# Hybrid two-layer encoder on one core: the first pass started from one row of c, with warm-up products on TensorE

## The chip, the cores and the metric

The kernel runs on one core of a Trainium2 chip. The core has five engines with an instruction queue each: TensorE (PE, with its weight loads shown apart as PEld), VectorE (DVE), ScalarE (ACT), GpSimd (POOL) and SyncE (SP), which here issues all DMA transfers. Each engine takes its instructions in the order in which the program was built; semaphores hold an instruction until what it needs is there. The metric is the device time of one execution in microseconds.

## The reference

The input x has 1024 tokens of 1024 features; c is one vector of 1024. Two layers follow each other, each with a modulation by c, and a last normalisation:

```
for i in range(2):
    mod = silu(c) @ ada_w[i] + ada_b[i];  shift, scale, gate = split(mod, 3)
    h = rmsnorm(x, norm_g[i]) * (1 + scale) + shift
    y = diff_attention(h, positions, ...) if i == 0 else mla(h, positions, ...)
    x = x + gate * y
return rmsnorm(x, final_norm_g)
```

Layer 0 projects h to q, k, v and z (each 1024 wide), turns q and k by rope (cosines and sines of position times frequency), forms two softmax maps per head (8 heads), subtracts lambda times the second, and gates by silu(z). Layer 1 is latent attention. All is float32.

## The kernel before

A float32 product on TensorE is made of three (`mm3`, lines 183 to 186): each operand is split into a high part in fp32r (a ScalarE copy) and a low part (a subtraction on GpSimd or VectorE), and high x high, high x low and low x high are added up in PSUM.

The first pass is what the change touches. The tokens are two halves of four tiles of 128. For the first half the kernel must have c: line 424 loads it spread to 128 partitions (512 KB) on SP's queue, ahead of the four tiles of x (line 524). ScalarE and VectorE form twice silu(c) (lines 427, 428) and ScalarE copies it into PSUM as `cb` (line 559). Squares of x (lines 534 on ScalarE, 537 on VectorE) lead to one root for the four tiles (`inv_rms`, line 465, GpSimd's power at line 171); ScalarE scales the first 256 features of each tile (line 567), VectorE the rest (line 621).

Then a loop goes over eight chunks k of 128 features. `mod_pair` multiplies two loaded tiles of ada weights (512 KB each, tag `ada`, four buffers) with `cb` and sums (line 434): the shift and scale of the chunk. `h_chunk` (line 479) transposes the chunk of the four token tiles on TensorE (line 488), ScalarE applies scale and shift twice (lines 493 to `h0h`, 495 to `h`), GpSimd subtracts (line 498) to `h0l`. `load_wv` (line 543) loads a chunk of value weights (tag `wvr`, two buffers) and splits it (lines 547, 548); every fourth chunk a strip of key weights (`wraw`, lines 208, 229, 230) is split too. Fifteen matmuls a chunk (lines 638 to 644) add to four value accumulators and one key accumulator: ten with `h0h`, then five with `h0l`. The matmuls of chunk k are issued one turn later than its `h_chunk` (`SKEW`).

Within the loop the second half of x is loaded (`X1_AT`), and the query weights (`WQ_AT`). In the last turn `angles()` runs: nine VectorE steps on a 128 x 256 tile, a table load and three sines on ScalarE, and three stores; `load_tables` brings the cosine and sine tables back in the layout of rope. After the loop the second half is squared and scaled, the query strip of the first half is multiplied, and the second half goes through the same chunks (lines 184 to 186 for its value matmuls). Then follow the value projection of the other heads (`vps`), the key and query strips of the second half, and the attention.

What sets the order: the program text gives work to the engines, and a list scheduler, by its own costs, orders each engine's queue when the program is built. `tc.issue_after(x)` keeps what is written under it behind x. The order is fixed before the kernel runs.

Of the kernel before, what the change touches and what calls it, by code (L numbers as in the profile page):

```python
# [11 lines left out]
F32 = mybir.dt.float32  # L12
# [52 lines left out]
WQ_AT = 6  # L65
# [3 lines left out]
X_CUT = 256  # L69
FIN_LAG = 1  # L70
# [15 lines left out]
def trunk(ctx: ExitStack, tc: tile.TileContext, A, out):  # L86
# [329 lines left out]
    def mod_load(src, mp, nb, tag="ada"):  # L416
        w = mp.tile([P, D], F32, name="ada", tag=tag, bufs=nb)
        SP.dma_start(w, src)
        return w

    def load_c(pl, th, **kw):

        c2 = pl.tile([P, D], F32, name="c2", **kw)
        SP.dma_start(c2, A["c"].to_broadcast([P, D]))

        def fin():
            S.activation(th, c2, AF.Tanh, scale=0.5)
            V.scalar_tensor_tensor(out=c2, in0=th, scalar=1.0, in1=c2, op0=ALU.add, op1=ALU.mult)

        return c2, fin  # L430
# [48 lines left out]
    def h_chunk(l, xn4, k, dst, hp, sub=G, wide=False, act=False, f32=None):  # L479
# [13 lines left out]
        S.activation(hh, tr[:, :n, :], AF.Identity, bias=bk, scale=ak)  # L493
        if act:
            S.activation(tmp, tr[:, :n, :], AF.Identity, bias=bk, scale=ak)
        else:
            V.tensor_scalar(tmp, tr[:, :n, :], ak, bk, op0=ALU.mult, op1=ALU.add)
# [16 lines left out]
    def load_x(half):  # L514

        xs = []
        for j in range(4):
            if half == 1 and j > 1:
                xs.append([wp.tile([P, HF], F32, name="xth", tag="rp", bufs=6) for _ in range(2)])
            else:  # L520
                xs.append([p1.tile([P, D], F32, name="xt", tag="xt", bufs=6)])
            for i, x_ in enumerate(xs[j]):
                n = D // len(xs[j])
                SP.dma_start(x_, A["x"][half * 4 + j, :, i * n : i * n + n])
        return xs

    def sq_x(xs, on_act=range(4)):
        ss = sm.tile([P, 4], F32, name="xss")
        for j, x_ in enumerate(xs):
            for i, piece in enumerate(x_):  # L530
                dst = ss[:, j : j + 1] if i == 0 else sm.tile([P, 1], F32, name="xs2")
                if j in on_act:
                    junk = p1.tile([P, D], BF16, name="junk", tag="junk", bufs=1)
                    S.activation(junk[:, : piece.shape[1]], piece, AF.Square, accum_out=dst)
                else:
                    junk = p1.tile([P, D], BF16, name="junk2", tag="h32", bufs=2)
                    V.tensor_tensor_reduce(out=junk, in0=piece, in1=piece, scale=1.0, scalar=0.0, op0=ALU.mult, op1=ALU.add, accum_out=dst)
                if i:
                    V.tensor_add(ss[:, j : j + 1], ss[:, j : j + 1], dst)
        return ss  # L540

    def load_wv(l, k, fh, src, eng=G):
        raw = p1b.tile([P, HF], F32, name="wvr", tag="wvr", bufs=2)
        SP.dma_start(raw, src)
        h_ = p1b.tile([P, HF], F32R, name="wvh", tag="wv", bufs=16)
# [5 lines left out]
    psum("ps1", accx=3, tr=1, cb=1)  # L551
    th = p1.tile([P, D], F32, name="cth", tag="ada", bufs=ADA_B)
    c2, c_fin = load_c(p1b, th)
    xs0 = load_x(0)
    posi = p1.tile([P, 256], I32, name="posi", tag="rot", bufs=3)
    SP.dma_start(posi, A["pos"])
    c_fin()
    cb = bank("cb", "cb", [P, D])
    S.copy(cb, c2)

    def ada0(j):
        return [mod_load(A["ada_ss0"][j, i], p1, ADA_B) for i in range(2)]

    wm0 = ada0(0)
    y0 = inv_rms(sq_x(xs0, X_ACT0), 4)
    for j in range(4):
        S.mul(xs0[j][0][:, :X_CUT], xs0[j][0][:, :X_CUT], y0[:, j : j + 1])


    tabS = [dr.tile([4, 32, 256], F32, name=f"tabS{i}") for i in range(3)]  # L570

    def angles():
        ang = p1.tile([P, 256], F32, name="ang", tag="rot", bufs=3)
        kk = p1.tile([P, 256], F32, name="kk", tag="rot", bufs=3)
# [12 lines left out]
        nsin = p1.tile([P, 256], F32, name="nsin", tag="h32", bufs=2)  # L587
        S.activation(kk, ang, AF.Sin, scale=0.5)
        S.activation(nsin, ang, AF.Sin, scale=-1.0)
        S.activation(ang, ang, AF.Sin)  # L590
        V.tensor_mul(kk, kk, kk)
        V.tensor_scalar(kk, kk, -2.0, 1.0, op0=ALU.mult, op1=ALU.add)
        for d_, s_ in zip(tabS, (kk, nsin, ang)):
            SP.dma_start(d_.rearrange("b p t -> (b p) t"), s_)
# [15 lines left out]
    for k in range(-1, KT + SKEW):  # L610
        if k + 1 < KT:
            wm = wm0 if k < 0 else ada0(k + 1)
            wv0.append(load_wv(0, k + 1, 0, A["w_v0"][k + 1, 0]))
            if k % 4 == 0:
                for d_, w_ in zip(wk0, load_strip([A["w_s0"][1, 0, k // 4]], [4])):
                    d_ += w_
            m_last = mod_pair(0, k + 1, wm, cb)
        if k < 0:
            with tc.issue_after(m_last):
                for j in range(4):  # L620
                    V.tensor_scalar(xs0[j][0][:, X_CUT:], xs0[j][0][:, X_CUT:], y0[:, j : j + 1], None, op0=ALU.mult)
        if k == KT - 1:
            with tc.issue_after(m_last):
                angles()
        if k == X1_AT:
            xs1 = load_x(1)
# [1216 lines left out]
```

## Time and profile before

| | us |
|---|---|
| runs | 1444.38, 1444.8, 1437.6 (median 1444.38) |
| the profiled execution | 1438.65 |
| its span | 1436.9 |
| TensorE busy | 1388.8 (97%) |
| VectorE, ScalarE, GpSimd busy | 917.5, 728.7, 610.6 |
| TensorE idle before its first transpose | 14.5 |

The profile is of one execution. A line of the timeline gives the start and the duration in microseconds, the engine, the program's line, the operation and its tiles (out, then in); what stands in brackets is the idle time in front of it and what ended it. Lines joined with xN follow each other without a break. A line of stretches gives its bounds and length, then busy time and number of instructions of PE, PEld, DVE, ACT and POOL, the granted clock, the busy share of the DMA engines and GB/s. A line of waits gives the total, the number and the longest. Matmuls are pipelined: their durations overlap, and the distance of two starts is what one costs.

### The profile page before, as it was taken

What the parts mean: (1) busy time and instruction counts of PE and PEld (TensorE: products, weight loads), DVE (VectorE), ACT (ScalarE), POOL (GpSimd) and SP (SyncE); (2) the same over time, 40 slices, a digit from 0 to 9 for tenths busy, and PEclk for the clock granted to TensorE, in tenths of its full rate; (3) what the DMA queues carried; (4) which work ended last, traced back from release to release, by engine and by line L of the source; (5) the groups of instructions that cost most, each with busy time, mean ns of one, the idle gap of its engine ahead of it and who ended that gap; (6) DMA issues with size and microseconds to landing.
All of it is one profiled execution on the core that took longest, in us unless ns stands there. A gap on an engine that the chain in (4) does not pass through costs nothing. (4 is left out here: it accounts for less than half of the span.)

```text
span 1436.9 us, 20644 instructions
## 1 busy us (share of the span) xinstructions
PE 1388.8 (97%) x7388; PEld 1158.8 (81%) x7388; DVE 917.5 (64%) x1372; ACT 728.7 (51%) x1287; POOL 610.6 (42%) x483
## 2 busy tenths in 40 slices
PE   5999999999999999998999999999999999999997
PEld 4778788888888888887787877887888888888886
DVE  6656877767777767677435985545666555555355
ACT  5622375666565656566343452335455554545342
POOL 4416164656464646464461343532141331412572
PEclk9999999999999999999999999999999999999999
DMA  8787723333332333237653145398343432336563
GB/s 326 238 254 237 255 70 93 84 104 81 96 101 84 96 89 91 86 96 248 236 183 125 38 132 184 122 305 236 133 130 111 130 101 77 104 96 217 185 237 136
DMA packets 135527, 213.70 MB, mean 149 GB/s; under 512 B 19072, under 2 KB 56064, under 8 KB 135424
## 3 DMA queue, kind: packets, MB, share of 16 engines
q1 hardware_dynamic: 135424, 212.38, 47.1%
q8 instruction: 58, 0.95, 0.3%
q14 instruction: 45, 0.37, 0.1%
HBM read 137.92 MB, written 50.80 MB: 131 GB/s over the span
## 5 line engine op out<-in xcount | busy, mean ns | idle before, releaser
L384 ACT CAST pth<-tr 128x512 fp32r<-128x512 f32 x256 | 150.6, 588 | 284.2 <-PE tr L382 281.9
L399 DVE TENSOR_REDUCE nm<-s 128x1 f32<-128x1024 f32 x192 | 234.1, 1219 | 77.2 <-PE s L773 65.7
L385 DVE TENSOR_TENSOR ptl<-tr,pth 128x512 fp32r<-128x512 f32 x256 | 176.2, 688 | 139.4 <-ACT pth L384 138.9
L230 POOL TENSOR_TENSOR wl<-wraw,wh 128x512 fp32r<-128x512 f32 (+2 forms) x79 | 103.6, 1314 | 205.6 <-ACT wh L229 183.4
L401 ACT ACTIVATE e<-s,nm 128x1024 f32<-128x1024 f32 x128 | 143.7, 1123 | 29.8 <-DVE nm L399 29.2
L382 PE MATMUL tr<-ident,e 128*128 128x128 f32 x1024 | 155.1, 274 | 2.3 <-DVE ptl L385 2.0
L382 PEld LDWEIGHTS tr<-ident,e 128*128 128x128 f32 x1024 | 121.2, 140 | 43.6 <-DVE ptl L385 19.2
L184 PE MATMUL acc<-h0h,wh 128*128 128x512 f32 x360 | 150.1, 417 | 1.9 <-DVE v_hl L362 1.8
L184 PE MATMUL pv<-pth,vt 128*128 128x256 f32 x512 | 147.1, 287 | 0.0
L185 PE MATMUL pv<-ptl,vt 128*128 128x256 f32 x512 | 145.8, 285 | 0.0
L186 PE MATMUL pv<-pth,vt 128*128 128x256 f32 x512 | 144.7, 283 | 0.0
L186 PE MATMUL acc<-h0h,wl 128*128 128x512 f32 x360 | 143.1, 398 | 0.5 <-POOL wl L230 0.5
L185 PE MATMUL acc<-h0l,wh 128*128 128x512 f32 x360 | 142.0, 394 | 0.0
L1013 POOL TENSOR_TENSOR wol<-wor,woh 128x512 fp32r<-128x512 f32 x64 | 85.0, 1351 | 84.7 <-ACT woh L1012 77.2
L185 PEld LDWEIGHTS pv<-ptl,vt 128*128 128x128 f32 x512 | 97.6, 191 | 2.9
L184 PEld LDWEIGHTS pv<-pth,vt 128*128 128x128 f32 x512 | 97.4, 190 | 2.9 <-ACT pth L384 0.2
L186 PEld LDWEIGHTS pv<-pth,vt 128*128 128x128 f32 x512 | 97.6, 191 | 0.1
L326 POOL TENSOR_TENSOR rp_r<-rp_raw,cosT 128x512 f32<-128x512 f32 x38 | 49.8, 1311 | 91.0 <-ACT rp_raw L321 50.8
L331 POOL TENSOR_TENSOR rp_sw<-rp_sw,sinT 128x512 f32<-128x512 f32 x42 | 55.4, 1318 | 74.1 <-DMA rp_sw<-rp_raw 73.9
L773 PE MATMUL s<-ks,qa 128*128 128x512 f32 x256 | 82.6, 404 | 2.8 <-DVE e L781 2.6
L781 DVE SCALAR_TENSOR_TENSOR e<-s,z,e 128x1024 f32<-128x1024 f32 x64 | 82.1, 1283 | 2.1
L773 PE MATMUL s<-ks,qb 128*128 128x512 f32 x256 | 81.1, 395 | 0.0
(590 smaller groups left out, 3335.4 us busy)
## 6 DMA issues: line engine op xcount, KB each, us to landing
ada<-in_ada_ss SPq DMA_DIRECT2D x32, 512.0 KB, 6.0
wraw<-in_w_s SPq DMA_DIRECT2D x64, 256.0 KB, 2.9
vS<-v_hl SPq DMA_DIRECT2D x32, 512.0 KB, 5.9
vt<-vS SPq DMA_DIRECT2D x32, 512.0 KB, 3.7
wor<-in_w_out SPq DMA_DIRECT2D x64, 256.0 KB, 3.9
rp_sw<-rp_raw SPq DMA_DIRECT2D x168, 64.0 KB, 2.0
bc_s<-bc_d SPq DMA_DIRECT2D x34, 256.0 KB, 4.1
oS<-bc_s SPq DMA_DIRECT2D x30, 256.0 KB, 2.5
```

The costliest lines, as they stand in the source:

```text
L184: PE.matmul(psum, ah, bh, start=first, stop=False)
L185: PE.matmul(psum, ah, bl, start=False, stop=False)
L186: PE.matmul(psum, al, bh, start=False, stop=last)
L230: sub = (V if pair_of else G).tensor_sub(l_[:, :n], raw[:, :n], f32v(h_[:, :n]))
L382: PE.transpose(tr[:, j, :], p[:, kt * P : (kt + 1) * P], ident)
L384: mk["S"] = S.copy(pth[kh][:, :, dst], tr).ins
L385: mk["V"] = V.tensor_sub(ptl[kh][:, :, dst], tr, f32v(pth[kh][:, :, dst])).ins
L399: mk["V"] = V.reduce_max(nm, s_ps, axis=AX.X, negate=True).ins
L401: mk["S"] = S.activation(e, s_ps, AF.Exp, bias=nm, scale=1.0, accum_out=zs).ins
L773: PE.matmul(s_ps[:, kc * HF : (kc + 1) * HF], src[:, c, ql], KS[h][kc][:, c, :], start=fst, stop=not fst)
L781: combined.append(V.scalar_tensor_tensor(out=e0, in0=e1, scalar=z1[:, 0:1], in1=e0, op0=ALU.mult, op1=ALU.add).ins)
L1013: in_turn(G.tensor_sub(lo, raw, f32v(hi)))
```

## The change

- c is loaded into one partition (`crow`, 4 KB). The tanh and the product with it work on that one row, and two f32 products of a row of ones with it (512 columns each) spread it to 128 partitions of `cb` in PSUM. The layer-1 copy `c2` is now made from `cb` in the loop.
- `keep_busy` adds 40 + 36 f32 products of ones by ones (128 x 128 x 128) into a bank of PSUM that nothing reads.
- The loads are reordered: position after the first tile of x, the first ada tile ahead of the fourth tile of x.
- The first three tiles of x get their root together; the fourth is squared in halves on ScalarE and VectorE and gets its own.
- The angle steps follow the product of c; the three sines stand behind chunks 2 and 3, the cosine's last two steps and the stores behind chunk 6 (`SIN_AT`).
- Value, key and query weights are loaded in one place and split in another, the split behind the chunk's last ScalarE step (`h_chunk.act`). `WQ_AT` goes from 6 to 5.
- The squares of the second half: two tiles on VectorE behind the last shift and scale, two on ScalarE behind the last chunk. Before, ScalarE did all.

In the order as built TensorE gets 55 of the 76 products first, then the two that spread c, then 21, then the first transposes. After the first pass the query strip of the second half now precedes its key strip. The last load of value weights for the next pass (the ninth `wvr`) stands ahead of the ada loads of chunk 7 on SP's queue.

```diff
-WQ_AT = 6
+WQ_AT = 5
+WARM = (40, 36)
+SIN_AT = (2, 3, 6)
...
-        c2 = pl.tile([P, D], F32, name="c2", **kw)
-        SP.dma_start(c2, A["c"].to_broadcast([P, D]))
...
+    warm = bank("acc", "warm")
+
+    def keep_busy(n):
+        for _ in range(n):
+            PE.matmul(warm[:, 0:P], ones, ones, start=True, stop=True)
+
+    crow = p1.tile([P, D], F32, name="crow", tag="ada", bufs=ADA_B)
     th = p1.tile([P, D], F32, name="cth", tag="ada", bufs=ADA_B)
-    c2, c_fin = load_c(p1b, th)
-    xs0 = load_x(0)
+    SP.dma_start(crow[0:1, :], A["c"])
+    xs0 = [load_x(0, 0)]
     posi = p1.tile([P, 256], I32, name="posi", tag="rot", bufs=3)
     SP.dma_start(posi, A["pos"])
-    c_fin()
-    cb = bank("cb", "cb", [P, D])
-    S.copy(cb, c2)
+    xs0 += [load_x(0, 1), load_x(0, 2)]
+    keep_busy(WARM[0])
...
+    wm0 = [ada0(0, 0)]
+    xs0.append(load_x(0, 3))
+    wm0.append(ada0(0, 1))
...
+    c_act = S.activation(th[0:1, :], crow[0:1, :], AF.Tanh, scale=0.5).ins
+    c_last = V.scalar_tensor_tensor(out=crow[0:1, :], in0=th[0:1, :], scalar=1.0, in1=crow[0:1, :], op0=ALU.add, op1=ALU.mult).ins
+    with tc.issue_after(c_last):
+        angles()
+    cb = bank("cb", "cb", [P, D])
+    for f in range(2):
+        fs = slice(f * HF, f * HF + HF)
+        PE.matmul(cb[:, fs], ones[0:1, :], crow[0:1, fs], start=True, stop=True)
+    keep_busy(WARM[1])
...
+    for j in range(3):
+        with tc.issue_after(c_act if j in X_ACT0 else c_last):
+            sq_piece(xs0[j][0], ss0[:, j : j + 1], j in X_ACT0)
+    y_ = inv_rms(ss0[:, 0:3], 3)
...
+    sq_halves([xs0[3][0][:, :HF], xs0[3][0][:, HF:]], ss0[:, 3:4])
+    y0[3] = inv_rms(ss0[:, 3:4], 1)[:, 0:1]
...
+    def sines(n):
+        with tc.issue_after(h_chunk.act):
+            if n == 0:
+                S.activation(kk, ang, AF.Sin, scale=0.5)
+                S.activation(nsin, ang, AF.Sin, scale=-1.0)
+            if n == 1:
+                S.activation(ang, ang, AF.Sin)
+                S.copy(c2, cb)
+        if n == 2:
+            with tc.issue_after(m_last):
+                V.tensor_mul(kk, kk, kk)
+                V.tensor_scalar(kk, kk, -2.0, 1.0, op0=ALU.mult, op1=ALU.add)
+            for d_, s_ in zip(tabS, (kk, nsin, ang)):
+                SP.dma_start(d_.rearrange("b p t -> (b p) t"), s_)
...
-            wm = wm0 if k < 0 else ada0(k + 1)
-            wv0.append(load_wv(0, k + 1, 0, A["w_v0"][k + 1, 0]))
+            wm = wm0 if k < 0 else [ada0(k + 1, i) for i in range(2)]
+            vraw = fetch_wv(A["w_v0"][k + 1, 0])
+            if k < 0:
+                with tc.issue_after(h_chunk.act):
+                    wv0.append(split_wv(vraw))
...
         if 0 <= k < KT:
             h_chunk(0, xs0, k, h0[k][0], p1, act=True)
+            if k + 1 < KT:
+                with tc.issue_after(h_chunk.act):
+                    wv0.append(split_wv(vraw))
+            if k in SIN_AT:
+                sines(SIN_AT.index(k))
...
-    norm_x(sq_x(xs1), xs1)
+    ss1 = sm.tile([P, 4], F32, name="xss")
+    with tc.issue_after(m_last):
+        for j in range(2):
+            sq_piece(xs1[j][0], ss1[:, j : j + 1], False)
+    with tc.issue_after(h_chunk.act):
+        for j in range(2, 4):
+            sx = sm.tile([P, 1], F32, name="xs2")
+            sq_piece(xs1[j][0], ss1[:, j : j + 1], True)
+            sq_piece(xs1[j][1], sx, True)
+            V.tensor_add(ss1[:, j : j + 1], ss1[:, j : j + 1], sx)
+    norm_x(ss1, xs1)
```

123 lines of the change are left out of this document (61 added, 62 removed).

## The prediction

> **What bounds the kernel now.** I read the page's first part, then TensorE's waits, then the busy time of each engine in stretches of the first 120 us, where every edit lies, and at last the timeline there. The issue order of the two programs, laid side by side, differs on all engines only up to about this time.
>
> ```profile
> span 1436.9 us, 20644 instructions
> PE 1388.8 (97%) x7388; PEld 1158.8 (81%) x7388; DVE 917.5 (64%) x1372; ACT 728.7 (51%) x1287; POOL 610.6 (42%) x483
> ...
> PE trh L488 <- ACT xt L567: 14.5, 1, 14.5
> ...
> 0.00:20.90 20.90, 5.53 (x15) 3.53 (x16) 12.19 (x21) 10.52 (x16) 6.43 (x11) 1.00 0.89 333
> 20.90:49.20 28.30, 28.10 (x134) 22.52 (x132) 21.99 (x44) 17.74 (x28) 18.08 (x15) 1.00 0.91 335
> 49.20:55.00 5.80, 3.62 (x8) 2.37 (x9) 2.53 (x6) 4.64 (x13) 1.26 (x1) 0.71 0.61 184
> 55.00:85.00 30.00, 29.57 (x143) 23.84 (x143) 19.51 (x33) 10.35 (x18) 8.63 (x7) 1.00 0.68 199
> 85.00:120.00 35.00, 32.92 (x139) 25.62 (x139) 20.93 (x30) 9.89 (x18) 11.57 (x7) 1.00 0.84 243
> ```
>
> TensorE is busy 97% of the span, so a microsecond counts if TensorE gets it. What the first pass can give is its idle time: 14.5 us before the first transpose, 2.2 us (5.80 less 3.62) around the last chunk, 2.1 us (35.00 less 32.92) later. Between 20.9 and 49.2 TensorE is full (28.10 of 28.30): there the pass can begin sooner but not run faster.
>
> ```profile
> 0.82 0.17 DVE L145 MEMSET ones<- 128x128 f32 x1 [0.82 <-PEq L1832]
> 1.17 0.42 SPq L424 DMA_DIRECT2D c<-in_c  x1
> 6.22 1.06 ACT L427 ACTIVATE cth<-c 128x1024 f32<-128x1024 f32 x1 [4.22 <-DMA c<-in_c]
> 12.87 1.28 DVE L434 CUSTOM_DVE_ANT_0 ada<-ada,cb,vec 128x1024 f32<-128x1024 f32 x1
> 14.46 1.68 PE L488 MATMUL trh<-ident,xt 128*128 128x128 f32 x4 [14.46 <-ACT xt L567]
> 15.43 0.16 DVE L442 SCALAR_TENSOR_TENSOR moda<-moda,vec 128x1 f32<-128x1 f32 x1
> 16.18 0.78 ACT L493 ACTIVATE h0h<-trh,modb,moda 128x512 fp32r<-128x512 f32 x1
> 17.01 0.80 PE L638 MATMUL vacc<-wvh,h0h 128*128 128x512 f32 x1 [0.87 <-ACT h0h L493]
> 20.15 0.63 PE L638 MATMUL vacc<-wvh,h0h 128*128 128x512 f32 x1
> 20.57 0.48 PE L639 MATMUL vacc<-wvl,h0h 128*128 128x512 f32 x1
> 20.89 0.40 PE L638 MATMUL vacc<-wvh,h0h 128*128 128x512 f32 x1
> 23.30 0.50 PE L638 MATMUL vacc<-wvh,h0h 128*128 128x512 f32 x1 [0.18 <-ACT h0h L493]
> 24.09 0.60 PE L488 MATMUL trh<-ident,xt 128*128 128x128 f32 x4
> 36.42 0.40 PE L638 MATMUL vacc<-wvh,h0h 128*128 128x512 f32 x1
> 36.65 0.40 PE L639 MATMUL vacc<-wvl,h0h 128*128 128x512 f32 x1
> 46.74 0.39 PE L638 MATMUL vacc<-wvh,h0h 128*128 128x512 f32 x1
> 51.28 1.93 PE L643 MATMUL vacc<-wvh,h0l 128*128 128x512 f32 x4 [2.10 <-POOL h0l L498]
> 54.75 0.47 PE L186 MATMUL acc<-h0h,wq 128*128 128x512 f32 x1
> 55.06 0.39 PE L184 MATMUL acc<-h0h,wq 128*128 128x512 f32 x1
> ```
>
> Two more costs show. Matmuls start 0.42 us apart at 20.15 to 20.57 and 0.23 apart at 36.42 to 36.65: TensorE is slow from its first work at 14.46 until 20.89 (6.4 us), and again from 51.28 until 54.75 (3.5 us) after the 2.10 us wait. And chunk 1 begins at 23.30, chunk 7 at 46.74: six chunks in 23.44 us, 3.91 each.
>
> **The yardstick.** The fourth matmul of the query strip starts at 55.06. If chunk 0's matmuls begin at S and nothing stalls, it starts at S + 7 x 3.91 + 18 x 0.23 = S + 31.5. So S = 23.6 would change nothing.
>
> **Warm-ups.** 76 f32 products of ones by ones are added. The text asks for 40, the row of c, then 36. In the changed program's issue order 55 stand ahead of the two products that spread c and 21 behind them, and the first transposes come after all. Their price is that of the like-shaped product in the tail:
>
> ```profile
> 703.37 1.13 PE L830 MATMUL rb<-sq,ones 128*128 128x128 f32 x8 [0.93 <-DVE sq L829]
> 704.25 0.48 PE L184 MATMUL oacc<-woh,oth 128*128 128x512 f32 x1
> ...
> 1350.48 1.05 PE L830 MATMUL rb<-dg,ones 128*128 128x128 f32 x8
> 1351.29 0.48 PE L184 MATMUL oacc<-woh,o1a3h 128*128 128x512 f32 x1
> ```
>
> Four products leave eight records, and the next instruction starts 0.88 or 0.81 us later: 0.20 to 0.22 us a product, taken as 0.21. 76 cost 16.0 us (15.4 to 16.7). The two spreading products have four times the columns: 0.84 each, 1.7 together; at the 0.23 of a 512-column record, two records each, it is 0.9. The slow stretch of 3.5 to 6.4 us loses about half: 1.7 to 3.2, taken as 2.5. TensorE can start when the ones are there, 1.0. So c is spread at 1.0 + 55 x 0.21 + 2.5 + 1.7 = 16.8, and the transposes start at T = 16.8 + 21 x 0.21 = 21.2, against 14.46 before (bounds 1.0 + 15.4 + 0.9 + 1.7 = 19.0 and 1.0 + 16.7 + 1.7 + 3.2 = 22.6).
>
> The Trainium skill, "TensorE: Matmul & The Clock Gate", section "Back-to-back issue gap", gives some 81 ns for a sustained matmul of 128 columns. By that estimate 76 cost 6.2 us and T is about 10; the rows above are of this shape and type and say 0.21, and I go by them.
>
> **c as a row.** The 4.6 us from issue (1.59) to use (6.22) of the 512 KB spread load, the copy into PSUM and the 128-row operand go; c is ready no later than there. It then waits behind the warm-ups until 16.8, so this earns nothing. It also holds a buffer: row and tanh take two of the four ada buffers, and the second shift/scale load of chunk 1 waits for the spreading products. Everything behind it on SP's queue waits too (key weights, next value weights, later ada). I expect transfers to run dry before that.
>
> **Shift and scale of chunk 0.** The first pair took 12.87 to 15.59, 2.7 us. Two angle steps now sit inside:
>
> ```profile
> 18.55 0.62 ACT L229 CAST wh<-wraw 128x512 fp32r<-128x512 f32 x1
> 46.36 1.34 DVE L585 SCALAR_TENSOR_TENSOR ang<-kk,ang 128x256 f32<-128x256 f32 x3
> 47.74 0.29 DVE L586 TENSOR_SCALAR ang<-ang 128x256 f32<-128x256 f32 x1
> 40.58 1.29 POOL L548 TENSOR_TENSOR wvl<-wvr,wvh 128x512 fp32r<-128x512 f32 x1 [0.28 <-ACT wvh L547]
> 55.19 0.64 ACT L534 ACTIVATE junk<-xth 128x512 bf16<-128x512 f32 x1
> 59.96 0.38 PE L488 MATMUL trh<-ident,xt 128*128 128x128 f32 x2
> 61.43 0.50 PE L184 MATMUL vacc<-wvh,h0h 128*128 128x512 f32 x1 [0.43 <-ACT h0h L493]
> ada<-in_ada_ss SPq DMA_DIRECT2D x32, 512.0 KB, 6.0
> wraw<-in_w_s SPq DMA_DIRECT2D x64, 256.0 KB, 2.9
> ```
>
> 0.45 + 0.29 more: ready at 16.8 + 3.5 = 20.3, ahead of the transposes (21.2 + 0.60 = 21.8). The key-weight split stands ahead of h0h on ScalarE: 16.8 + 2.9 for the transfer, up to 1.5 more for the 512 KB in front at 335 GB/s, + 0.62 = 20.3 to 21.8, just covered. Then h0h and first matmul, 16.18 to 17.01: S = 21.8 + 0.8 = 22.6 (bounds 20.4 and 24.0). By the yardstick that gains 1.0.
>
> **Last tile, squares, sines, angles.** The separate fourth tile and the angle steps lie on ScalarE and VectorE before 17 and are covered by the warm-ups; were these gone, the angle steps inside the first pair would cost their 0.7. The sines, one table load and the copy of c for layer 1 go between chunks 2 and 5 on ScalarE; each chunk of 3.91 us asks 2.2 us of it (0.78 + 0.78 + 0.62), so they fit in what is left over. This clears the path of the last h32, and the 2.10 us wait with the slow stretch (half of 3.5) goes. That gain is already in the yardstick. What is late next: SP's order puts the value weights of the next pass ahead of chunk 7's shift and scale; their buffer is freed by GpSimd's split of chunk 6. That follows h0l of chunk 5, whose transposes stand at chunk 4: 22.6 + 15.6 + 0.4 + 0.78 + 0.78 = 40.2; GpSimd is then still on the key-weight subtraction (1 us left, I estimate from its three in a row of 1.29), then h0l and the split, 1.29 each: about 43.7. Two stores of sines stand in that stretch of SP's queue too. The two 512 KB loads issue then and land 2.9 to 6.0 later (I take 4.3, the queue being short) and 1.5 more (512 KB at 335 GB/s): 49.5; a product and the scale 1.5, h0h 0.8: chunk 7 starts at 51.8 and not 22.6 + 27.4 = 50.0. A stall of 1.8 (0.3 to 3.5). The yardstick falls at 55.9, 0.8 late (bounds -3.2 with no stall and S 20.4; +5.9 with S 24.0, 3.5 and another 1.8 of slow clock).
>
> **Second half of the tokens.** Its loads follow chunk 7's on SP: 2 MB at 335 GB/s end at 55.8; from the last square to the transposes it took 4.8 us (55.19 to 59.96) and to the first matmul 6.2: 62.0 against 61.43, and the strip, 0.8 late, asks the same. I carry +0.8. The query strip now precedes the key strip, and only 5 of the value matmuls stand before it; weights are wanted later. Of the 2.1 us idle in 85 to 120 I save half (0 to 2.1).
>
> **Sum.** +0.8 - 1.0 = -0.2 on the profiled execution's 1438.65 (span 1436.9 and 1.75 around it): 1438.5. The runs lie on two levels, 1437.6 with the profile and 1444.4 to 1444.8; the median, 1444.38, is 5.7 above it. I name 1441, between 1438.5 and 1444.2, which is the same sum on the median. 0.5% (7.2 us), the spread of these runs, is what a measurement tells from no change.
>
> **Rivals.**
> - Slower: the clock stays shut during f32 products. For it: after the transposes it opened only 3.9 us behind the first fp32r matmul (17.01 to 20.89), and no trace here has f32 products for microseconds on end. Against: 6.4 us from the first transpose fits as well. Then 76 x 0.21 x 0.42 / 0.23 = 29.1, spread 3.1, T = 33.2, S = 34.6, 1.8 more until it opens: 67.9 at the yardstick, with the same stall 69.7, +14.6; less 1.0: 1452.2. Above half that excess it decides. Chance 0.09.
> - Faster: the warm-ups overlap so well that they no longer hold c back. S is then set by the shift and scale; VectorE has more ahead of them than before, so no sooner than 12.87: 12.87 + 3.5 + 0.8 = 17.2, 6.4 gained, 1432. Against it stand both rb rows, where a product would have to cost half. 0.05. (The skill's 81 ns, from the section named above, would do this.)
> - The upper level of the runs comes from the spread load of c, which took 4.6 us for the first bytes; one row of 4 KB ends it. All runs would be near 1438, 0.45% under the median. No row speaks of the upper level. 0.10.
> - Chunk 7's stall at its long end with the slow clock: +5, 1443.7, on the upper level 1449. 0.10.
>
> **How the numbers follow.** The forecast has 0.66. Range 1433 to 1450: it takes in all but the shut clock and the cheap warm-ups (0.14) and some scatter. Faster by over 0.5%: 0.13 (cheap warm-ups, most of the level case with a microsecond gained, little else). Slower: 0.13 (shut clock, some of the long stall). Same: 0.74.
>
> **What would show it.** The first transpose of xt near 21 and the products for cb ending near 17, not 6; warm-up records 0.1 apart after 4 to 8 us; chunk 0 near 22.6; no wait for h0l at chunk 7, but one for its h0h with VectorE waiting for ada; the strip's fourth matmul at 53 to 58. A first chunk before 20 or after 27 would prove the first step wrong.

## The result, and the profile after

The changed kernel takes 1448.47 us (median of 14 runs, 1445.85 to 1450.48); the kernel before, in runs between these on the same chip, 1441.63 us (14 runs, 1437.6 to 1445.33). The ratio is 1.0043, 95% interval 1.0031 to 1.0055: about 6 us slower. That is outside the interval and inside the 0.5% that the prediction had set aside; the forecast of no change (-0.2 us) was wrong. The profiled executions stand 7.9 us apart, 1446.54 (span 1444.8) against 1438.65; the traces below are of these two executions, and show some 1.7 us more than the ratio.

The first part of the page after:

```profile
span 1444.8 us, 20958 instructions
PE 1408.7 (98%) x7544; PEld 1179.8 (82%) x7544; DVE 924.9 (64%) x1378; ACT 725.4 (50%) x1285; POOL 610.2 (42%) x484
```

TensorE is busy 19.9 us longer than before (1408.7 against 1388.8), about what the warm-up products take (14.07 and 6.58 us in the timeline below). Busy time alone says nothing here: the kernel now computes ones by ones.

The busy time of each engine in stretches, after (start:end, length, then PE, PEld, DVE, ACT, POOL, each with its count, the granted clock of TensorE, DMA share and GB/s):

```profile
0.00:20.90 20.90, 19.86 (x136) 18.50 (x137) 10.87 (x29) 7.58 (x13) 3.70 (x9) 0.93 0.73 250
85.00:120.00 35.00, 32.44 (x135) 25.94 (x133) 22.25 (x31) 9.19 (x16) 9.12 (x5) 0.95 0.82 245
120.00:150.00 30.00, 29.40 (x130) 24.03 (x128) 15.78 (x24) 10.12 (x17) 16.62 (x11) 1.00 0.68 203
150.00:180.00 30.00, 24.93 (x108) 19.71 (x109) 22.60 (x35) 8.71 (x15) 0.89 (x1) 1.00 0.91 283
...
17.91:21.32 3.41, 3.41 (x18) 3.41 (x18) 3.41 (x9) 0.00 (x0) 0.00 (x0) 0.50 1.04 295
...
93.00:96.41 3.41, 3.41 (x10) 2.63 (x9) 2.83 (x5) 0.00 (x0) 0.00 (x0) 0.50 0.84 241
```

The same view of before, for the two stretches that the prediction did not look at:

```profile
120.00:150.00 30.00, 30.00 (x134) 24.84 (x133) 20.09 (x31) 9.28 (x16) 14.12 (x9) 1.00 0.85 273
150.00:180.00 30.00, 28.66 (x135) 22.87 (x134) 24.19 (x35) 12.62 (x23) 3.83 (x3) 1.00 0.74 233
```

The last stretch is the surprise: between 150 and 180 us, far behind every edit, TensorE is busy 24.93 us where it was 28.66, with 108 matmul records where there were 135. And within these 180 us the clock, once open, was shut twice for 3.41 us, once among the warm-ups themselves.

The timeline of after at the places that matter (start, length, engine, line, what; in brackets the idle time before it and what ended that; SPq is SyncE's queue of transfers):

```profile
1.04 14.07 PE L551 MATMUL warm<-ones 128*128 128x128 f32 x110 [1.04 <-DVE mhalf L168]
15.04 1.98 PE L593 MATMUL cb<-crow,ones 1*128 1x512 f32 x4
16.95 6.58 PE L551 MATMUL warm<-ones 128*128 128x128 f32 x42
23.37 0.60 PE L479 MATMUL trh<-ident,xt 128*128 128x128 f32 x4
24.84 0.50 PE L688 MATMUL vacc<-wvh,h0h 128*128 128x512 f32 x1 [0.87 <-ACT h0h L484]
38.52 4.39 SPq L210 DMA_DIRECT2D wraw<-in_w_s  x2
45.20 0.33 SPq L533 DMA_DIRECT2D wvr<-in_w_v  x1
45.63 0.85 SPq L420 DMA_DIRECT2D ada<-in_ada_ss  x2
49.84 1.28 DVE L425 CUSTOM_DVE_ANT_0 ada<-ada,cb,vec 128x1024 f32<-128x1024 f32 x1 [2.81 <-DMA ada<-in_ada_ss]
53.47 0.50 PE L688 MATMUL vacc<-wvh,h0h 128*128 128x512 f32 x1 [1.15 <-ACT h0h L484]
58.48 0.39 PE L186 MATMUL acc<-h0h,wq 128*128 128x512 f32 x1
64.83 0.50 PE L186 MATMUL vacc<-wvh,h0h 128*128 128x512 f32 x1 [0.43 <-ACT h0h L484]
92.28 0.50 PE L186 MATMUL acc<-h0h,wq 128*128 128x512 f32 x1 [2.11 <-DVE v_hl L364]
122.28 0.59 ACT L363 CAST v_hl<-vps 128x512 fp32r<-128x512 f32 x1 [6.07 <-PE vps L188]
122.76 0.62 ACT L345 CAST ks<-rp_r 64x512 fp32r<-64x512 f32 x1
132.21 4.81 SPq L210 DMA_DIRECT2D wraw<-in_w_s  x2
143.28 0.63 SPq L366 DMA_DIRECT2D vS<-v_hl  x1
150.93 0.58 ACT L363 CAST v_hl<-vps 128x512 fp32r<-128x512 f32 x1 [17.22 <-DMA vS<-v_hl]
152.29 0.50 PE L186 MATMUL vps<-wvh,h0h 128*128 128x512 f32 x1 [2.89 <-DVE v_hl L364]
168.48 0.50 PE L186 MATMUL acc<-h0h,wh 128*128 128x512 f32 x1 [1.71 <-DVE v_hl L364]
```

and the rows of before that answer to its last third:

```profile
106.20 0.59 ACT L361 CAST v_hl<-vps 128x512 fp32r<-128x512 f32 x1
113.16 0.61 ACT L343 CAST ks<-rp_r 64x512 fp32r<-64x512 f32 x1
126.49 3.86 SPq L208 DMA_DIRECT2D wraw<-in_w_s  x2
136.55 0.63 SPq L364 DMA_DIRECT2D vS<-v_hl  x1
142.41 0.59 ACT L361 CAST v_hl<-vps 128x512 fp32r<-128x512 f32 x1 [13.21 <-DMA vS<-v_hl]
159.65 0.50 PE L184 MATMUL acc<-h0h,wh 128*128 128x512 f32 x1 [1.13 <-DVE v_hl L362]
```

Three rows make an account of the loss, because the work between them is the same in both programs (from H to A both traces hold 420 matmul records, of the same tiles): S, the first matmul of chunk 0; H, the first matmul of the second half of the tokens; A, the first `acc<-h0h,wh` behind the first attention scores.

| | S | H | A | profiled time |
|---|---|---|---|---|
| before | 17.01 | 61.43 | 159.65 | 1438.65 |
| after | 24.84 | 64.83 | 168.48 | 1446.54 |
| late | +7.8 | +3.4 | +8.8 | +7.9 |

The chunks win back 4.4 us, as was meant. Between H and A the changed kernel takes 103.65 us where the one before takes 98.22. TensorE's waits there are 2.11, 0.45, 2.89, 0.27 and 1.71, in sum 7.4, and the clock shut at 93.00 costs half of 3.41; before, the waits are 0.65, 0.65, 0.22, 0.47 and 1.13, in sum 3.1. The difference, 6.0, is the 5.4 within 0.6 us. Behind A the changed kernel is 0.9 us quicker.

Two queues stand out. On SyncE, the query weights (`wraw`, 38.52 to 42.9, of which 3.4 us wait for GpSimd's split to free a buffer) and a ninth value load (45.20) stand ahead of the shift and scale of chunk 7 (45.63): the wait at 53.47. On ScalarE, the eviction of the second half's value tile 0 (122.28) stands ahead of the casts of the keys (122.76) and waits 6.07 us for TensorE. The tile takes 24 matmuls. Before, 22 of them stood ahead of the query strip and the rest right behind it; the tile was finished at 106.20, and the casts came at 113.16. In the changed kernel 5 stand ahead of the key strip, 12 behind it, and the last 7 only behind the 48 matmuls of two more strips (108.83 to 120.45). From there the lateness goes on through the weight load on SyncE (132.21 against 126.49), the store of the values (143.28 against 136.55) and the eviction that it holds up (150.93 against 142.41), into TensorE's wait of 2.89. The eviction is not all that holds the casts, though: e5 and e13 show a second wait, on VectorE, that ends at nearly the same time.

### The profile page after: what moved, and what is told of

Read it like the earlier page. It is cut to its first block, busy times and chain, and to the rows that moved or that the text cites. A ratio compares the mean times of both kernels' runs of the same rounds, so it can differ in the third digit from the quotient of the medians.

```text
span 1444.8 us, 20958 instructions
## 1 busy us (share of the span) xinstructions
PE 1408.7 (98%) x7544; PEld 1179.8 (82%) x7544; DVE 924.9 (64%) x1378; ACT 725.4 (50%) x1285; POOL 610.2 (42%) x484
## 5 line engine op out<-in xcount | busy, mean ns | idle before, releaser
L333 POOL TENSOR_TENSOR rp_sw<-rp_sw,sinT 128x512 f32<-128x512 f32 x42 | 56.5, 1346 | 76.2 <-DMA rp_sw<-rp_raw 74.7
```

## The experiments

The short names: "fetch" is the turn of the loop at which the query weights are fetched and split (`WQ_AT`), and with it their place in SyncE's queue, "casts" the place of the key casts in ScalarE's. The letters in the expectations were given to the theories one after another: A the warm-ups, B the order of the two strips, C the fetch, D the casts, E that TensorE itself or the loads are late and no queue, F the turn of the accumulator banks, G the open clock, H the casts as the larger of the two queues. All times are medians, ratios against the kernel before in the same session.

**e1_nowarm: no warm-ups.**

```diff
-WARM = (40, 36)
+WARM = (0, 0)
```

> All 76 warm-up products are left out, nothing else is edited. Theory A (the warm-ups stand in front of c and of the first transposes, and what they delay reaches the end): c is spread by about 9, the shift and scale are ready near 18, chunk 0 begins near 19 instead of 24.84, and the fourth matmul of the query strip, at 58.48 in the changed kernel, at 52 to 54; the clock opens only after chunk 0 has begun. The time falls by 4 to 7 us against the changed kernel, to 1442 to 1445, level with the kernel before or up to 3 us slower. Theory B (the loss is made later, by the new order of the strips and by SP's queue, whatever the first pass does): chunk 0 is earlier as well, but the time falls by less than 2 us.

1445.9 us, 1.0040 [1.0027, 1.0053]: as slow as with them. Its timeline:

```profile
17.11 0.78 DVE L583 SCALAR_TENSOR_TENSOR ang<-kk,ang 128x256 f32<-128x256 f32 x1
...
19.46 0.78 ACT L484 ACTIVATE h0h<-trh,modb,moda 128x512 fp32r<-128x512 f32 x1 [3.19 <-DVE moda L433]
...
20.29 0.80 PE L688 MATMUL vacc<-wvh,h0h 128*128 128x512 f32 x1 [4.00 <-ACT h0h L484]
...
149.85 0.50 PE L186 MATMUL vps<-wvh,h0h 128*128 128x512 f32 x1 [2.54 <-DVE v_hl L364]
```

The warm-ups hold chunk 0 back by 4.5 us (24.84 against 20.29). But without them it still starts 3.3 us later than before: TensorE waits 4.00 us for h0h, and h0h for VectorE, which now does angle steps and the scaling of three token tiles ahead of the products of shift and scale, and angle steps between them. At H (62.78) 2.0 us of the 4.5 are left, and from H to A (166.61) this kernel takes as long as the changed one (103.83 against 103.65): the wait at 149.85 is still there. Theory A is not the whole.

**e4_warm72: 36 more.** `WARM = (40, 72)`.

> 36 warm-up products more (40 + 72), behind the spread of c. Theory A: each costs 0.225 us in full, 36 cost 8.1; chunk 0 begins near 32.9 and the time rises by 6 to 9 us, to 1455 to 1457. Theory B (an absolute chain on SP's queue sets the time near 150): the rise is under 4 us.

1458.6 us, 1.0130 [1.0112, 1.0148]. Chunk 0 starts 7.7 us later than after:

```profile
32.56 0.50 PE L688 MATMUL vacc<-wvh,h0h 128*128 128x512 f32 x1 [0.87 <-ACT h0h L484]
```

and the end is later by some 12.5 us (1.0130 less 1.0043), more than the 6 to 9 expected; where the rest arises was not followed. So a delay at the beginning does reach the end, when it is as long as this.

**e2_fullrow: c spread by 128 rows, not one**, to see whether the one-row products shut the clock at 17.91.

```diff
+    G.memset(crow, 0.0)
-        PE.matmul(cb[:, fs], ones[0:1, :], crow[0:1, fs], start=True, stop=True)
+        PE.matmul(cb[:, fs], ones, crow[:, fs], start=True, stop=True)
```

> c is spread by two products over all 128 rows (the other 127 rows of the c tile are set to zero first) instead of one row; the 76 warm-ups stay. Theory A with the clock: the 1.9 us of one-row products do not count as work for the clock gate, so it shut from 17.9 to 21.3 in the changed kernel; with full rows it stays open, the 21 products behind c take 4.7 us instead of 6.4, chunk 0 begins near 23.1, and the time falls by 1.7 us (1.0 to 2.5). Rival (the gate shut by the pause at a boundary or by chance of the window): the 21 products still take 6.4 us and the time is the same within 1 us.

1446.54 us, 1.0048 [1.0036, 1.0061]: no gain. The clock stayed open near 18 us here, and chunk 0 began at 23.32, near the 23.1 expected; yet H came at 68.80, behind a wait of 3.17 for chunk 7. The clock stayed open too in the profiles of e4, e5, e6 and e7, which keep the one-row products, and was shut at 18.65 in that of e3, which keeps them as well. These two shuttings, in the changed kernel and in e3, are, but for the end of an execution, the only ones ahead of which the traces show no wait, and both come about 1 us behind the 1.98 us of one-row products; a wait of some 2 us, too, shut the clock in some executions and not in others (the last section). So they may have shut it; that they did is not shown.

**e3_kfirst: the key strip ahead of the query strip again, in the second half**, by an order of issue:

```diff
+            with tc.issue_after(after[0]) if after else nullcontext():
+                gen_half.last = mm3(acc, hi[k], lo[k], rh, rl, k == 0, k == n - 1)
...
-    for i, _ in enumerate(gen_half(wq0, h0, 1, lambda acc: q_done(0)(acc, 1))):
+    for i, _ in enumerate(gen_half(wq0, h0, 1, lambda acc: q_done(0)(acc, 1), [k_last])):
```

> The changed kernel with one constraint more: the query strip of the second half is kept behind its key strip, as in the kernel before. The first pass is the same: chunk 0 near 24.8, the strip's fourth matmul near 58.5. Theory B: the 2.11 us wait in front of the query strip at 92 with the 3.4 us of slow clock behind it goes, the key and query rope reach SP's queue sooner, the stores of values near 150 come 3 to 5 us sooner, and the time falls by 3 to 5 us, to 1443.5 to 1445.5. Theory A alone: what is late near 150 is late because the first pass is, and the time falls by less than 1.5 us.

1449.53 us, 1.0068 [1.0053, 1.0082]. It made a wait of its own,

```profile
100.79 0.79 PE L186 MATMUL acc<-h0h,wh 128*128 128x512 f32 x1 [9.69 <-DVE v_hl L365]
```

and so neither speaks for theory B nor against it; e9 and e12 ask the same without such a wait.

**e5_ksfirst: casts ahead of the eviction on ScalarE.**

```diff
-            S.copy(t[64:128, 1, :], r[64:128])
+            stack_k.last = S.copy(t[64:128, 1, :], r[64:128]).ins
...
+        with tc.issue_after(after) if after is not None else nullcontext():
             S.copy(v[:, 0, :], acc)
...
-            store_v(0, p1b, acc, tt, fh)
+            store_v(0, p1b, acc, tt, fh, after=stack_k.last if tt == 0 else None)
```

> The changed kernel with one wait taken out of ScalarE's order: the eviction of the first value tile of the second feature half (v_hl from vps, tile 0) is put behind the four key casts (ks) instead of ahead of them. Theory D (a blocked queue at 116 to 122 us sets the end): in the changed kernel ScalarE waits 6.07 us for that tile at 122.28, the key casts that were ready at about 116 come at 122.76, GpSimd's subtractions at 123.52, the strip fetch on SyncE at 132.21 and the value evictions at 150.93. With the order turned, the casts start at 116 to 119, the fetch at 126 to 129, the 2.89 us wait of TensorE for v_hl at 152 is under 1.5 us, and the kernel is 3 to 7 us faster than the changed one (ratio to before 0.999 to 1.002). Rival E (what is late at 150 us is late because TensorE itself or the loads are late): the casts move and the time stays within 1.5 us of the changed kernel (ratio 1.003 to 1.006).

1446.22 us, 1.0040 [1.0023, 1.0057]: a miss, no gain can be seen. The casts did not come sooner:

```profile
125.65 0.62 ACT L345 CAST ks<-rp_r 64x512 fp32r<-64x512 f32 x1 [5.68 <-DVE modb L426]
```

Something else held ScalarE, a product of shift and scale on VectorE (`modb`). In this execution the first pass had itself ended 6.4 us late (H at 67.81, with a chunk-7 wait of 2.42), so the wait that was removed had another one behind it. In the changed kernel the same product ends only 0.9 us ahead of its casts (122.76):

```profile
121.77 0.08 DVE L425 DVE_READ_ACCUMULATOR2_ANT modb<- 128x1 f32 x1
```

If they wait for it there as here, the eviction alone held them back by no more than that.

**e6_wq6: the query fetch one chunk later.** `WQ_AT = 5` to `6`.

> The changed kernel with the fetch of the query strip put back to chunk 6, behind the ada tiles of chunk 7 on SyncE. Theory C (the query strip's fetch, which holds SyncE from 38.52 to 42.9 us, makes chunk 7 late): the dots of chunk 7 start 2 us or more earlier than 49.84, TensorE's 1.15 us wait for h0h at 53.47 is gone, and the fourth matmul of the query strip comes at 56.5 to 57.8 instead of 58.48. On the end it is worth 0 to 2 us, since by theory D the stretch from 116 us on has its own bound. Rival: the ada tiles wait for their buffers and not for the queue; then chunk 7 is as late as it was, within 0.5 us.

1446.08 us, 1.0033 [1.0019, 1.0048]. The wait of chunk 7 is gone, as expected, and little comes of it alone: TensorE waits 1.44 us at the query strip instead (57.38), whose fourth matmul starts at 58.18 and not at 56.5 to 57.8, and H (64.44) is only 0.4 us sooner. The edit also moves the ninth value load behind the shift and scale of chunk 7, so it does not tell the two loads apart.

**e7_kw: e5 and e6 together.**

> Both edits, the key casts ahead of the eviction and the query strip's fetch at chunk 6, warm-ups kept. Theories C and D together: 4 to 9 us faster than the changed kernel, ratio to before 0.997 to 1.001. Rival E: within 2 us of the changed kernel.

1443.01 us, 1.0019 [1.0009, 1.0029]: 3.4 us faster than the change (1.0043 less 1.0019), a little less than the 4 to 9 expected. Now both queues run as they should:

```profile
39.08 1.53 SPq L421 DMA_DIRECT2D ada<-in_ada_ss  x2
44.42 1.28 DVE L426 CUSTOM_DVE_ANT_0 ada<-ada,cb,vec 128x1024 f32<-128x1024 f32 x1 [0.20 <-DMA ada<-in_ada_ss]
115.93 0.60 ACT L345 CAST ks<-rp_r 64x512 fp32r<-64x512 f32 x1
139.63 0.59 ACT L364 CAST v_hl<-vps 128x512 fp32r<-128x512 f32 x1 [8.43 <-DMA vS<-v_hl]
163.40 0.50 PE L186 MATMUL acc<-h0h,wh 128*128 128x512 f32 x1 [1.33 <-DVE v_hl L365]
```

The shift and scale of chunk 7 leave at 39.08, not 45.63; the casts come at 115.93, not 122.76; the eviction at 139.63, not 150.93, and TensorE's wait of 2.89 is gone. A is 3.8 late, and H (64.66) 3.2: what is left was there at the start.

**e8_kwn: e7 without warm-ups.**

> Both edits and no warm-up matmuls. With the chain behind 116 us out of the way what the warm-ups cost ahead of it should reach the end: chunk 0 at about 20.3 us as without warm-ups before, and 1.5 to 3 us faster than the kernel with both edits and warm-ups (theory A, that the 76 warm-ups cost about 2 us net of what the open clock saves). If the warm-ups cost nothing the two agree within 1 us. Ratio to before 0.994 to 0.999.

1439.29 us, 0.9997 [0.9985, 1.0009]: equal to the kernel before, and 3.7 us faster than e7 (1.5 to 3 expected).

```profile
60.98 0.50 PE L186 MATMUL vacc<-wvh,h0h 128*128 128x512 f32 x1 [0.65 <-ACT h0h L485]
...
159.66 0.50 PE L186 MATMUL acc<-h0h,wh 128*128 128x512 f32 x1 [0.68 <-DVE v_hl L365]
```

H is 0.5 ahead of before, A equal to it (159.65). The three causes together hold the whole loss; all else that the change does neither costs nor earns anything that these runs can tell.

**e9_b_turn1: the kernel before, its accumulator banks shifted by one** (the warm-up tile takes a turn in their rotation; this takes it without the tile). `turn = 1` added behind the layout of the banks.

> The kernel before with one edit: the rotation of the accumulator banks starts one place later, as it does in the changed kernel, where the warm-up tile takes the first place. No matmul is added. TensorE's order then has the query strip of the second half ahead of the key strip, as in the changed kernel. Theory F (the flip of the two strips, which the warm-up tile's bank brings about, makes the key casts and with them the chain behind 116 us late): the key strip ends about 33 matmuls of 0.23 us, 7 us, later, the value evictions come 2 us or more later than 142.41, and the kernel is 2 to 6 us slower than before (ratio 1.0014 to 1.004). Rival: the order of the two strips is worth nothing by itself, and the time stays within 1 us (0.9993 to 1.0007).

1438.68 us, 0.9988 [0.9978, 0.9998]. The query strip comes ahead of the key strip here too, so the warm-up tile's turn is what flips them; but the kernel is not slower for it. Theory F falls, and the trace shows why: here 9 matmuls of the value tile stand ahead of the key strip and the other 15 right behind it, so that the tile and the casts are as early as before.

```profile
105.51 0.59 ACT L361 CAST v_hl<-vps 128x512 fp32r<-128x512 f32 x1
112.61 0.61 ACT L343 CAST ks<-rp_r 64x512 fp32r<-64x512 f32 x1
```

The flip by itself costs nothing here; what differs from the changed kernel is where the tile's matmuls stand. One more thing is in this profile: its last-chunk wait is the 2.10 us of before, and the clock did not shut behind it:

```profile
49.20:55.00 5.80, 3.22 (x12) 2.04 (x13) 2.39 (x6) 4.79 (x13) 1.27 (x1) 1.00 0.67 196
```

where the row of before that the prediction quotes has 0.71.

**e10_b_warm42: the kernel before with 42 warm-ups in its idle time**, ahead of the first transpose, so that they displace nothing.

```diff
+    warm = bank("acc", "warm")
+    turn = 0
+    for _ in range(42):
+        PE.matmul(warm[:, 0:P], ones, ones, start=True, stop=True)
```

> The kernel before with 42 warm-up matmuls in TensorE's idle time ahead of its first transpose (14.46 us), the rotation of the banks set back, so that the order behind them is as before. They should be over by 12 to 14 us. Theory G (the open clock is worth what it says when it delays nothing): the clock opens at 4 to 7 us instead of 20.75, the transposes and chunk 0 run at full speed, and the kernel is 1 to 3 us faster than before (ratio 0.998 to 0.9993). Rival: the first pass is bound by the loads and dots, and waits of TensorE take the place of the slow clock; within 0.7 us of before.

1441.48 us, 1.0007 [0.9992, 1.0021]: nothing. The clock's records, in the windows view:

```profile
5.77:16.01 10.24, 8.46 (x68) 7.51 (x67) 7.07 (x13) 6.48 (x12) 1.04 (x1) 1.00 1.03 415
16.01:22.84 6.83, 5.89 (x15) 4.41 (x16) 6.80 (x10) 3.07 (x5) 5.97 (x4) 0.50 0.86 313
```

The clock opened at 5.77 and shut again at 16.01, between the warm-ups and the first chunk (16.75). Theory G, that an open clock at chunk 0 is worth 1 to 3 us, got no test here, since chunk 0 did not run at the open clock.

**e11_fit: e8, and 45 warm-ups placed where TensorE waits** (9 ahead of the spread of c, 24 behind it, 12 behind the transposes of chunk 0).

```diff
-WARM = (40, 36)
+WARM = (9, 24, 12)
...
+    with tc.issue_after(cb_last):
+        keep_busy(WARM[1])
...
+            if k == 0:
+                with tc.issue_after(h_chunk.tr):
+                    keep_busy(WARM[2])
```

> The kernel with both repairs (key casts first, query strip fetched at chunk 6) and the warm-ups fitted to TensorE's gaps: 9 ahead of the spread of c (over at about 5 us), 24 behind it (over at 13), 12 between the transposes of chunk 0 and its first matmul. Theory A and G: c is spread at about 7.5, the transposes come at 13.1 to 15.7 as without warm-ups, chunk 0 at 18.5 to 20.0 with the clock open, the fourth matmul of the query strip at 51.5 to 53.5, and the kernel is 1.5 to 3 us faster than the one without warm-ups, ratio to before 0.9965 to 0.9985. Rival: the first pass is bound by the loads and dots and takes the gain back; within 0.7 us of the one without warm-ups (0.999 to 1.000).

1440.55 us, 1.0001 [0.9992, 1.0010]: a miss. Chunk 0 did run at the open clock, but it started at 21.17 and not at 18.5 to 20.0, since the 24 warm-ups behind the spread held the first transposes until 16.77 (13.09 in e8). And

```profile
55.61 0.33 PE L480 MATMUL trh<-ident,xt 128*128 128x128 f32 x1 [1.37 <-DVE xt L469]
...
159.71 0.50 PE L186 MATMUL acc<-h0h,wh 128*128 128x512 f32 x1
```

A is where it was before (159.65) and in e8 (159.66). The transposes of chunk 4 are 0.6 us ahead of those of e8 (32.79 against 33.43), those of chunk 5 behind them (37.65 against 37.32), after a wait of 0.81; later TensorE waits for the scaled tokens of the second half (1.37). What an open clock at chunk 0 is worth when the warm-ups delay nothing, no run shows.

**e12_fit_turn0: e11 with `turn = 0`**, so that the key strip comes first again.

> As the fitted kernel, and the rotation of the accumulator banks set back, so that the key strip goes ahead of the query strip again. If the key casts' place alone was the trouble (theory D), it agrees with the fitted kernel within 1 us. If the order of the strips costs by itself (theory F), it is 1 to 3 us faster.

1442.29 us, 1.0009 [0.9997, 1.0021], beside e11's 1.0001: slower by 1.7 us, more than the 1 us expected and the other way than theory F has it. The order of the strips as before earns nothing here either.

**e13_nk, e14_nw6: one queue left, no warm-ups.** e13 is e8 with the fetch as in the change, e14 e8 with the casts as in the change.

> No warm-ups and the key casts ahead of the eviction, the query strip's fetch left at chunk 5. The two chains of the first 165 us, TensorE's and the one of the evictions, end together in the kernel before; a part that delays only one of them shows only when nothing delays the other. Theory H (blocked ScalarE queue is the larger of the two remaining causes): the evictions at 158 to 163 as before, ratio to before 0.9995 to 1.0015. If the fetch on SyncE is the larger one: 1.002 to 1.004.

> No warm-ups and the query strip's fetch at chunk 6, the eviction left ahead of the key casts. Theory H: the last evictions at 164 to 168 instead of 161, TensorE's wait for v_hl at about 150 us as long as 2 to 3 us, ratio 1.002 to 1.004. If the fetch on SyncE was the larger cause: 0.9995 to 1.0015.

e13 1445.52 us, 1.0027 [1.0015, 1.0040]; e14 1443.44 us, 1.0015 [1.0006, 1.0024]. Neither came as theory H expected: leaving the fetch costs 0.0030 on e8, leaving the casts 0.0018. But e13 does not leave the fetch alone. Its casts stand ahead of the eviction and still come late, behind the product on VectorE that held them in e5:

```profile
121.00 0.62 ACT L345 CAST ks<-rp_r 64x512 fp32r<-64x512 f32 x1 [5.67 <-DVE modb L426]
```

In e8 they come at 112.53, in e14, which leaves them, at 120.44. So with the fetch at chunk 5 the edit of the casts does not move them (why they must wait for that product then was not found), and the 0.0030 is the price of the fetch and of late casts together. Which of the two is larger stays open.

**e15_kw40: e7 with only the warm-ups ahead of the spread.** `WARM = (40, 0)`.

> Both repairs, 40 warm-ups ahead of the spread of c and none behind it. If only the warm-ups behind the spread cost (they hold the transposes until 23 us), the spread of c comes at 10 to 12 us, ahead of the first dot that VectorE can start at 15, the transposes come at 13 to 16, chunk 0 at 19.5 to 20.5, and the time agrees with the kernel without warm-ups: ratio 0.999 to 1.001. If the warm-ups ahead of the spread cost too: 1.001 to 1.002.

1440.21 us, 0.9997 [0.9987, 1.0008], as expected: of the warm-ups only those behind the spread cost, since only they keep the transposes waiting (14.22 here; chunk 0 at 19.89, in e7 at 24.39). The clock had opened and was shut again over chunks 0 and 1:

```profile
15.80:26.04 10.24, 6.15 (x16) 4.79 (x17) 9.08 (x18) 4.43 (x7) 5.98 (x6) 0.50 0.93 324
```

In this one execution A is 161.60, 1.9 us behind e8; in the median of the runs no harm shows.

**Together.** With the three edits made or not (S, H, A and the first key cast from one execution each, the ratio from all runs):

| left as in the change | ratio | S | H | first key cast | A |
|---|---|---|---|---|---|
| all (the change) | 1.0043 | 24.84 | 64.83 | 122.76 | 168.48 |
| fetch, casts (e1) | 1.0040 | 20.29 | 62.78 | 120.67 | 166.61 |
| fetch, warm-ups (e5; the casts late all the same) | 1.0040 | 24.50 | 67.81 | 125.65 | 170.04 |
| casts, warm-ups (e6) | 1.0033 | 24.15 | 64.44 | 121.71 | 165.91 |
| fetch (e13; the casts late all the same) | 1.0027 | 19.66 | 65.88 | 121.00 | 165.30 |
| warm-ups (e7) | 1.0019 | 24.39 | 64.66 | 115.93 | 163.40 |
| casts (e14) | 1.0015 | 19.57 | 61.14 | 120.44 | 164.38 |
| none (e8) | 0.9997 | 19.68 | 60.98 | 112.53 | 159.66 |

With the fetch repaired the other two add up, within the noise: the casts cost 0.0018 (e14) or, beside the warm-ups, 0.0014; the warm-ups 0.0022 (e7) or, beside the casts, 0.0018. With the fetch left as in the change they show less or not at all: taking out the warm-ups gives 0.0003 (e1), or 0.0013 from e5 to e13, and the edit of the casts does not move the casts (e5). The fetch is worth 0.0025 without warm-ups (e1 less e14), 0.0010 with them (the change less e6). So taking one cause away from the full set gives 0.0010 at most, though all three cost 0.0046 over e8. For the casts the trace shows what hid them, the wait on VectorE. For the warm-ups it is argued, not shown: chains that run beside each other meet at the evictions ahead of A, and the latest counts. The ratios are good to some 0.001 each, too little to prove that the warm-ups cost less beside the fetch than without it. The first fault found explains nothing until the others are gone.

What stays open: why TensorE's wait for `v_hl` at the first strip of the second half (2.11 in after, 0.65 in before) varies from 0.62 (e15, e11) over 1.53 (e8) to 3.17 (e5). No edit here governs it. It also stays open what the fetch costs when the casts are early. And no kernel tried is faster than before by as much as 0.5%; the fastest is e9, 0.9988.

## Why the prediction was wrong

**Right, by its own terms.** c was spread by 16.95 (16.8 forecast). Warm-ups cost 0.225 us each at the open clock: 42 records, 21 products, from 16.95 to 23.37, less half of the 3.41 of shut clock; 0.21 was taken. The yardstick of S + 31.5, with the stall of 1.8 put in, gave S + 33.3, and it was S + 33.6 (58.48 less 24.84); that is in part luck, since the wait before chunk 7 was 1.15 and not 1.8, and 0.50 at the query strip (57.67), which the sum does not have, came on top. The wait for h0l is gone, and SyncE's order puts a wait before chunk 7 in its place: VectorE waits for ada just as said. The prediction named the value load ahead of it; the query fetch stands there too, for longer (4.39 us). And the angle steps inside the first pair were covered by the warm-ups; e1 shows what they cost without cover: with the scaling ahead of them, chunk 0 starts at 20.29 though its last transpose starts at 15.82.

**Mis-sized.** S was 24.84, not 22.6, above the upper bound of 24.0. Of the 2.2 us, 1.7 are the second shutting of the clock, in the middle of the warm-ups, and 1.1 the price of 76 products (0.015 x 76); the first slow stretch gave 0.9 back (half of 1.04 to 4.26 is 1.6, and 2.5 was taken). The first slow stretch is read from the distance of the records, 0.21 us until 4.20 and 0.11 later. It is not the luck of one shutting: in e5, e6 and e7 the clock opened some 2 us later and did not shut again, and S is 24.15 to 24.50. H came 2.8 us later than forecast (64.83 against 62.0). The upper bound at the yardstick adds up to +5.7 and not to +5.9; +3.4 lies within both.

**The step that failed: the Sum, which ends at 120 us.** "The issue order of the two programs, laid side by side, differs on all engines only up to about this time", and for the second half "I carry +0.8", less half of 2.1 us of idle time. That the order is the same afterwards does not mean that the work stands where it stood. The prediction saw that the query strip now precedes the key strip with only 5 of the value matmuls ahead of it, and drew from it that "weights are wanted later". It did not ask who waits for that value tile: its eviction stands on ScalarE ahead of the key casts, in both kernels, and with the tile 16 us later (122.28 against 106.20) the casts, SyncE's queue and the evictions behind them are late as well. That this costs is shown by e14 against e8 (0.0018); that the casts have a second wait close behind, on VectorE, came out only in e5 and e13. From H to A the forecast was -1.0 and the trace says +5.4: 2.89 from the wait at 152.29, which is gone in e7; 3.2 from the longer wait at 92.28 (2.11 against 0.65) and the clock shut behind it (half of 3.41); the other waits cancel. The 2.1 us of idle time, of which half was to be saved, became 2.56 (35.00 less 32.44).

Lateness is read at points before which both programs have done the same work. Single matmuls, such as the value tile's own, stand at different places in the two orders and would mislead.

**The rivals.** The shut clock during f32 products did not happen; the products ran at 0.225 us and opened the clock at 4.26. The cheap warm-ups did not happen either. The upper level of the runs does not come from the spread load of c: without it the runs still lie from 1445.85 to 1450.48. The long stall with the slow clock did occur, in e2 (3.17), e5 (2.42) and e13 (3.24), all with the fetch as in the change. In the changed kernel's own profile it was 1.15 us, and it is not the loss by itself.

**The median.** 1441 was named from runs with a median of 1444.38. The fourteen runs, with these three among them, have 1441.63, so the foot it stood on was 2.75 too high; against that median, the sum would have said 1441.4. The two levels that the prediction saw in three runs are not there in fourteen, which lie spread from 1437.6 to 1445.33.

## What to carry to other kernels

When an order flips, follow each delayed tile to the engine that evicts it and ask what stands behind that eviction in the engine's queue: the price appears there, here 60 us later. The flip itself may be free, as in e9. A change with several small faults can hide each of them from an experiment that repairs one; repair them all first, put them back one at a time, and see in the trace that each edit moved what it was meant to move (that of e13 did not). Products that only keep TensorE busy cost their full time as soon as a needed product is issued behind them, and should end before its operands are ready.

## What the runs showed of the hardware

The clock shuts and opens in whole steps: every shut stretch recorded was 3.41, 6.83 or 10.24 us long, but for the last of each execution, which its end cuts. Ahead of the first opening there is no record, and the profile shows 1.00; only the distance of the matmuls tells that it is shut there. It shut behind single waits as short as 1.15 us (in the changed kernel, at 840 us) and 2.11 us, and, at 17.91 in the changed kernel and at 18.65 in e3, with no wait before it in the trace; while the same wait of 2.10 us in the first pass shut it in the kernel before and in e10, and not in e9. That fits the Trainium skill, "TensorE: Matmul & The Clock Gate", section "What's actually happening", which tells of a free-running window of 3413 ns: the lengths agree. It does not fit the advice of the same page of the Trainium skill, section "Why this matters for your kernels", to have no idle gaps over about 3 us: here the clock shut behind gaps well under that, though no run shows that the gap alone did it.

In the runs that start with 40 or more warm-ups the clock opened at 4.26 to 7.01 us, that is 3.2 to 6.0 us after the first of them. The section "Why this matters for your kernels" of that page of the Trainium skill asks for 4 us or more of continuous work to reach the full clock; these runs fit that roughly. But I had not expected that to be worth nothing: e10 (1.0007), e11 (1.0001) and e15 (0.9997) equal the kernel before. In e10 and e15 the clock shut again before the first chunk; in e11 the warm-ups delayed chunk 0 by 1.5 us against e8, and what the open clock won back was waited away at later transposes.
